# Sums of weight blocks in the second MLP product: accumulating transfers in place of GpSimd additions

## The chip, the core and the metric

The kernel runs on one core of a Trainium2 chip. Its engines work beside each other, each through its own queue in order: TensorE (PE; its weight loads are listed as PEld), VectorE (DVE), ScalarE (ACT), GpSimd (POOL), and SyncE (SP), which here only issues transfers. 16 DMA engines carry the transfers. The metric is the device time of one execution in microseconds.

## The reference

One encoder block in float32, 1024 tokens of width 1024: RMS norm, one combined projection, 2-D neighbourhood attention and a gated convolution, their gated merge, and an MLP. What the change touches is the last line, the second product:

```
h = rms_norm(x, norm2_g[l]) @ w_mlp_in[l]
x = x + jnp.square(jax.nn.relu(h)) @ w_mlp_out[l]
```

`w_mlp_out` is 4096 x 1024.

## The kernel before

Every product is made of float16 pairs: an operand is scaled, split into a high and a low half, and three passes (high x high, high x low, low x high) add up in PSUM. The big products also use a scheme of seven block products for 2 x 2 blocks in place of eight. It needs sums of blocks on both sides.

For the second MLP product the work is cut into four slices s = 0 to 3 of the inner dimension. A slice has four weight blocks w11, w12, w21, w22, each two tiles of 128 x 1024 float32 (512 KB each): w11 and w12 in four buffers `raw`, w21 and w22 in one buffer `w2x`. SP loads them from `in_weights`. The seven weight operands of a slice stand in `ORDER`: w11, then t2 = w12 + w22 + w11, then w21, then t3 = w12 + w22, then t1 = w11 + w12, then t4 = t2 + w21, then w22. t3 and t1 are made in place, in w12's and w11's buffers; t2 has a tile of its own (in slice 0 the second half of a tile `h0`, shown as h in the profile; later `t2`, shown as t). The activation sides, squared relu values and their sums, were stored to DRAM (`hs`) by the first product; they come back as `hf`, in four buffers in turn, three operands ahead (`h_load`, L1711).

`prep2(s)` makes the operands. For each one: ACT makes the high half of hf (L1765), DVE its low half (L1767); ACT makes the high half of the two weight tiles (L1770), DVE the low ones (L1776). Three operand buffers `ops` go round: `gate(i)` holds operand i back until PE is through with operand i - 3. Then follows the sum that a later operand needs: after w11, w11 += w12 (L1781, for t1); after t2, w12 += w22 (L1785, for t3); after t3, t2 += w21 (L1789, for t4). t2 is begun at the slice's start (L1739, L1740).

The consumer is the loop over 28 operands n = 7 s + o: four groups of 12 matmuls (L210), 128 x 512 each, one per 128 rows; DVE or ACT adds each result from PSUM (eight banks) to `acc` (L1866, L1864) or to the output tile `x1` (L1875). In slice 3 `combine` (L1837 to L1846) adds acc to the output on GpSimd and DVE.

The order of instructions on each engine is fixed at build time. The preparing functions are Python generators; at each matmul group the builder advances the one in front by four steps (`tick`). A `yield` is thus a place in the order and no wait. `prep2(s + 1)` stands behind `prep2(s)`. Waits come from the data alone: an instruction waits, at the head of its engine's queue, for the semaphores of what it reads or overwrites, and what stands behind it on the engine waits too.

Slice 0's preparation overlaps the end of the first product, whose sixteen quarters q leave results in tiles `as`: ACT applies relu and square (L1623, L1625), GpSimd makes four sums (L1345), SP stores them to hs (L1636).

Of the kernel before, what the change touches and what calls it, by code (L numbers as in the profile page):

```python
# [15 lines left out]
OP = mybir.AluOpType  # L16
# [36 lines left out]
def encoder_block(ctx: ExitStack, tc: tile.TileContext, x, weights, cols, gqk, rel, masks, out):  # L53
    nc = tc.nc
    V, A, G, T, SP = nc.vector, nc.scalar, nc.gpsimd, nc.tensor, nc.sync
# [27 lines left out]
    def cols_of(kind, n):  # L83
        a = area[kind]
        if a[1] + n > a[2]:
            assert kind != "keep"
            a[1] = a[0]
        a[1] += n
        return slice(a[1] - n, a[1])

    def keep(n=1):
        return cols_of("keep", n)
# [4 lines left out]
    def at(c, i, n=1):  # L97
        return slice(c.start + i, c.start + i + n)

    def mul(a, b, out=None):  # L100
        out = out or tmp(a.stop - a.start)
        V.tensor_tensor(sc[:, out], sc[:, a], sc[:, b], op=OP.mult)
        return out
# [126 lines left out]
    def load_into(t, ch, p):  # L230
        m = ch.widths[p][0] * ch.widths[p][1]
        n = m // (1 + (ch.half == 0 and p == 1))
        for o in range(0, m, n):
            SP.dma_start(t[:, o:o + n], bass.AP(tensor=weights.tensor, offset=weights.offset + ch.offs[p] + o,
                                                ap=[[m, 128], [1, n]]))

    def load_upto(n):
        while loaded[0] < min(n - held[0], limit[0], len(loads)):
            ch, p = loads[loaded[0]]
            loaded[0] += 1  # L240
            t = rawp.tile([128, 1024], F32, name="raw")
            load_into(t[:, :ch.widths[p][0] * ch.widths[p][1]], ch, p)
            ch.raw.append(t)
# [97 lines left out]
    for (kind, j), pieces in plan():  # L341
# [4 lines left out]
        for p, (k, w) in enumerate(ch.widths):  # L346
            ch.offs.append(offset)
            if kind != "X" and (kind, j) != ("1", 0) and (kind, j, p) != ("1", 1, 1):
# [3 lines left out]
    cV, cConv, cA, cB, cO, c1, c2, c2x = ([chunks[k, j] for j in range(n)] for k, n in  # L352
                                              (("V", 2), ("C", 4), ("A", 4), ("B", 4), ("O", 2),
                                               ("1", 16), ("2", 4), ("X", 4)))
# [687 lines left out]
    for k in range(N + 16):  # L1042
        p, w = k // 16, k % 16
# [71 lines left out]
    def sum_of(sm):  # L1115

        b, a = cols_of("prep", 1), ones_col()
        V.tensor_reduce(sc[:, b], sc[:, sm], axis=AX, op=OP.add)
        V.tensor_copy(a, sc[:, b])
        return a, work[0]  # L1120

    def scale_of(am, more, n=3):

        a, mark = am
        yield from apart(mark, n * 6144, work)
        b, s, inv = cols_of("prep", 1), cols_of("prep", 1), keep()
        yield from all_sum(a, b, anybank(), 1e-36)
        yield from pow2_half(b, 14, s, inv, more)
        return s, inv
# [277 lines left out]
    def gate(i):  # L1407
        while pe_done[0] < i - 2:
            yield
# [292 lines left out]
    def w2x_load(s):  # L1702
        pool = later["pool"] if s == 1 else wsp
        X2[s] = pool.tile([128, 4, 1024], F32, name="w2x", tag="w2x" if s == 1 else "ws", bufs=1 if s == 1 else 2)
        for i in range(4):
            load_into(X2[s][:, i], c2x[s], i)

    def h_load(n):
        s, f = n // 7, ORDER[n % 7][0]
        later["h", n] = later["hf"][:, n % 4]  # L1710
        SP.dma_start(later["h", n], HS[s][:, f])  # L1711
# [3 lines left out]
    def prep2(s):  # L1715
        raw, x2 = c2[s].raw, X2[s]
        w11, w12 = raw[0:2], raw[2:4]
        w21, w22 = [x2[:, i] for i in range(2)], [x2[:, i] for i in range(2, 4)]
        while not r_ready[s]:
            yield  # L1720
        Rs, iR = R[s]
        sm = cols_of("prep", 6)
        if s == 0:
            yield from gate(16)
            OPS[16] = TAGS[16 % 3][0].tile([128, 2, 2, 2048], F16, name="ops", tag=TAGS[16 % 3][1])
            j = OPS[16][:, 0, 0].bitcast(BF16)
        else:
            j = later["junk"]
        for i in range(4):
            A.activation(j[:, :1024], raw[i], AF.Square, scale=sc[:, iR], accum_out=sc[:, at(sm, i)])  # L1730
            yield
        for i in range(2):
            A.activation(j, x2[:, 2 * i:2 * i + 2].rearrange("p a c -> p (a c)"), AF.Square, scale=sc[:, iR],
                         accum_out=sc[:, at(sm, 4 + i)])
            yield
        sums = sum_of(sm)
        T2 = later["t2"]()
        for i in range(2):
            G.tensor_tensor(T2[:, i], w12[i], w22[i], op=OP.add)  # L1739
            G.tensor_tensor(T2[:, i], T2[:, i], w11[i], op=OP.add)  # L1740
        yield
        if s == 0:
            yield from gate(17)
            P = OPS[17] = TAGS[17 % 3][0].tile([128, 2, 2, 2048], F16, name="ops", tag=TAGS[17 % 3][1])
            later["h", 1] = P[:, 0].rearrange("p w m -> p (w m)").bitcast(F32).rearrange("p (k t) -> p k t", k=4)
            SP.dma_start(later["h", 1], HS[0][:, ORDER[1][0]])
        sw, inv = yield from scale_of(sums, 0)
        fw = keep()
        mul(iR, sw, fw)
        c2[s].inv = inv  # L1750
        yield
        for o, (f, name) in enumerate(ORDER):
            n = 7 * s + o
            i = 16 + n
            yield from gate(i)
            pool, tag = TAGS[i % 3]
            if n > 1:
                OPS[i] = pool.tile([128, 2, 2, 2048], F16, name="ops", tag=tag)
            P = OPS[i]
            while ("h", n) not in later:  # L1760
                yield
            if 1 < n < 25:
                h_load(n + 3)
            hf = later.pop(("h", n)).rearrange("p k t -> p (k t)")
            A.activation(P[:, 1, 0], hf, AF.Copy, scale=sc[:, Rs])  # L1765
            yield
            V.scalar_tensor_tensor(P[:, 1, 1], hf, sc[:, Rs], P[:, 1, 0], op0=OP.mult, op1=OP.subtract)  # L1767
            w = {"w11": w11, "t1": w11, "t3": w12, "w21": w21, "w22": w22}.get(name) or [T2[:, i] for i in range(2)]
            for i2 in range(2):
                A.activation(P[:, 0, 0, 1024 * i2:1024 * i2 + 1024], w[i2], AF.Copy, scale=sc[:, fw])  # L1770
            yield
            while i == 17 and pe_done[0] < 16:
                yield
            for i2 in range(2):
                sl = slice(1024 * i2, 1024 * i2 + 1024)
                V.scalar_tensor_tensor(P[:, 0, 1, sl], w[i2], sc[:, fw], P[:, 0, 0, sl], op0=OP.mult, op1=OP.subtract)  # L1776
                yield
            ready.add(i)
            if name == "w11":
                for i2 in range(2):  # L1780
                    G.tensor_tensor(w11[i2], w11[i2], w12[i2], op=OP.add)  # L1781
                yield
            elif name == "t2":
                for i2 in range(2):
                    G.tensor_tensor(w12[i2], w12[i2], w22[i2], op=OP.add)  # L1785
                yield
            elif name == "t3":
                for i2 in range(2):
                    G.tensor_tensor(T2[:, i2], T2[:, i2], w21[i2], op=OP.add)  # L1789
                yield  # L1790
            elif name == "t1":
                done[0] += 4
                load_upto(done[0] + 5)
                if s < 3:
                    w2x_load(s + 1)
                    bg.append(prep2(s + 1))
            yield
# [8 lines left out]

    bg.append(first2())
    bg.append(prep2(0))
    whole(14)
    whole(15)  # L1810
# [39 lines left out]
    for n in range(28):  # L1850
        s, o = n // 7, n % 7
# [92 lines left out]
```

## Time and profile before

| | |
|---|---|
| median of 2 runs | 1206.88 us (1206.52 to 1207.23) |
| profiled execution, span from first to last instruction | 1205.3 us |
| PE busy | 1188.0 us (99%) |
| DVE busy | 938.7 us (78%) |
| ACT busy | 759.8 us (63%) |
| POOL busy | 433.1 us (36%) |
| DMA | 173.36 MB, mean 144 GB/s |

The profiled execution's own time is the span; what lies around it isn't shown apart, and the median of the runs is 1.6 us longer. A row of a group names line, engine, operation, output and inputs, shapes and count; then busy us and the mean ns of one; then the idle time of the engine just before, and what ended it. A row of the timeline has start, duration, engine, line, operation, count, and in brackets the idle time before it with its releaser. Rows of waits and brackets put a wait for several things down to the one that came last.

### The profile page before, as it was taken

To read this page: it belongs to the slowest core of one execution; us is meant where nothing else is said; L and a number is where in the kernel's file an instruction comes from. 1 tells how busy PE (TensorE), PEld (TensorE's weight loads), DVE (VectorE), ACT (ScalarE), POOL (GpSimd) and SP (SyncE) were. 2 spreads that over 40 slices of the span, in tenths; PEclk is the share of its full clock that TensorE was granted. 3 is DMA by queue.
4 is the path that set the end of the run, shared out by engine and by line. 5 is a ranking of instruction groups with operands and counts; after the bars stand their busy time and mean duration, and the time that the engine had idled before them with its cause. 6 is when DMAs were issued, how large, how long until landed. Compare 5 with 4: busy or idle time off the path is not lost.

```text
span 1205.3 us, 17076 instructions
## 1 busy us (share of the span) xinstructions
PE 1188.0 (99%) x6294; PEld 573.8 (48%) x6294; DVE 938.7 (78%) x1759; ACT 759.8 (63%) x1183; POOL 433.1 (36%) x280
## 2 busy tenths in 40 slices
PE   6999999999999999999999999999999999999998
PEld 4444445555444444444467444444444444444444
DVE  7777988988368787877878655545548999999997
ACT  7766679867554545337779778678676744746440
POOL 1640011222311112001004465565567471553662
PEclk9999999999999999999999999999999999999999
DMA  7766657676542211224386545445465925334202
GB/s 264 151 213 141 140 119 130 133 146 123 103 123 65 67 56 53 70 93 187 57 155 183 182 159 192 149 139 193 145 247 201 352 97 217 129 138 194 105 35 105
DMA packets 171012, 173.36 MB, mean 144 GB/s; under 512 B 131504, under 2 KB 132016, under 8 KB 166832
## 3 DMA queue, kind: packets, MB, share of 16 engines
q1 hardware_dynamic: 170352, 168.07, 47.9%
q10 hardware_dynamic: 576, 4.19, 0.8%
q8 instruction: 49, 0.80, 0.3%
q14 instruction: 35, 0.29, 0.1%
HBM read 102.51 MB, written 37.75 MB: 116 GB/s over the span
## 4 chain that ended last, share of the span: by engine, by line
PE 73%; DVE 9%; ACT 1%; issue 1%; DMA 1%; DVEq 0%; ACTq 0%
PE ps_d L210 26%; PE ps_s L210 23%; PE ps_o L210 16%; PE ps_d L1039 6%; DVE w_s L1163 2%; PE ps_o L1016 1%; PE ps_s L959 1%; DVE sg L1279 1%; DVE P L999 1%; DMA u2T<-v 1%; DVE sz L973 1%; ACT w_s L1167 0%; DVE sc L317 0%; DVE m L1281 0%; ACT sg L1245 0%
## 5 line engine op out<-in xcount | busy, mean ns | idle before, releaser
L210 PEld LDWEIGHTS <-ops 128*128 128x128 f16 x1356 | 132.4, 98 | 157.3
L210 PEld LDWEIGHTS <-w 128*128 128x128 f16 x1368 | 132.8, 98 | 140.0 <-DMA u2T<-v 0.6
L1039 PE MATMUL ps_d<-uT,w_ws 128*128 128x512 f16 x528 | 123.7, 379 | 0.1
L210 PE MATMUL ps_d<-ops 128*128 128x512 f16 (+1 forms) x528 | 118.3, 374 | 0.0
L1765 ACT ACTIVATE ops<-hf,sc 128x2048 f16<-128x2048 f32 x26 | 52.0, 2000 | 97.9 <-PE ps_o L210 35.2
L210 PE MATMUL ps_s<-ops 128*128 128x512 f16 x492 | 112.9, 379 | 0.0
L1152 POOL TENSOR_TENSOR tsum<-raw 128x512 f32<-128x512 f32 x28 | 46.0, 1658 | 149.6 <-ACT raw L1138 141.6
L1345 POOL TENSOR_TENSOR as<-as 128x512 f32<-128x512 f32 x56 | 77.5, 1384 | 39.3 <-ACT as L1625 36.0
L210 PEld LDWEIGHTS <-w_s 128*128 128x128 f16 x588 | 56.8, 98 | 69.4 <-DVE w_s L1163 1.9
L210 PE MATMUL ps_d<-u2x,w 128*128 128x512 f16 (+1 forms) x360 | 80.0, 372 | 0.0
L210 PEld LDWEIGHTS <-uT 128*128 128x128 f16 x504 | 49.0, 98 | 59.6 <-DMA uT<-u 0.8
L1039 PEld LDWEIGHTS <-w_ws 128*128 128x128 f16 x528 | 51.2, 98 | 54.5 <-DVE cv L861 0.4
L210 PE MATMUL ps_o<-ops 128*128 128x512 f16 x336 | 77.1, 379 | 0.0
L1767 DVE SCALAR_TENSOR_TENSOR ops<-hf,sc,ops 128x2048 f16<-128x2048 f32 x26 | 74.0, 2846 | 3.7 <-ACT ops L1765 3.7
L210 PE MATMUL ps_o<-u2T,w 128*128 128x512 f16 (+1 forms) x324 | 71.7, 371 | 0.0
L1138 ACT ACTIVATE raw<-raw,sc 128x256 f32<-128x256 f32 x172 | 71.0, 493 | 0.8 <-DMA raw<-in_weights 0.7
L1152 POOL TENSOR_TENSOR gsum<-raw 128x512 f32<-128x512 f32 x14 | 19.0, 1376 | 133.0 <-issue 72.8
L1167 ACT ACTIVATE w<-raw,sc 128x512 f16<-128x512 f32 (+1 forms) x28 | 24.6, 927 | 54.1 <-DVE sc L426 54.1
L297 DVE SCALAR_TENSOR_TENSOR w_ws<-raw,sc,w_ws 128x512 f16<-128x512 f32 (+2 forms) x72 | 51.2, 763 | 4.7 <-ACT w_ws L306 4.7
L1658 DVE TENSOR_TENSOR as<-ps_d,as 128x512 f32<-128x512 f32 (+1 forms) x14 | 9.4, 672 | 55.8 <-ACT as L1677 53.4
L210 PE MATMUL ps_s<-u2T,w 128*128 128x512 f16 (+1 forms) x252 | 52.7, 359 | 0.0
L982 ACT ACTIVATE sz<-sz,sc 128x384 f32<-128x384 f32 (+1 forms) x64 | 37.2, 582 | 22.5 <-DVE sc L973 15.0
(357 smaller groups left out, 2629.5 us busy)
## 6 DMA issues: line engine op xcount, KB each, us to landing
raw<-in_weights SPq DMA_DIRECT2D x88, 512.0 KB, 5.4
hs<-as SPq DMA_DIRECT2D x16, 1792.0 KB, 8.7
hf<-hs SPq DMA_DIRECT2D x26, 1024.0 KB, 6.3
w2x<-in_weights SPq DMA_DIRECT2D x16, 512.0 KB, 8.1
raw<-in_weights SPq DMA_DIRECT2D x16, 384.0 KB, 3.5
xt<-in_x SPq DMA_DIRECT2D x8, 512.0 KB, 10.0
gs<-s ACTq DMA_DIRECT2D x4, 1024.0 KB, 4.0
x<-in_x SPq DMA_DIRECT2D x8, 512.0 KB, 9.8
```

Of the source, the lines that this page charges most:

```text
L210: T.matmul(ps, l, r, start=a, stop=b)
L297: V.scalar_tensor_tensor(lo, self.raw[p][:, o:o + m], sc[:, c:c + 1], hi, op0=OP.mult, op1=OP.subtract)
L959: T.matmul(ps[:, :nb * 128], QD[:, p, e, w, i * 128:(i + 1) * 128], KD[:, 2 * p + e, lo * 128:(lo + nb) * 128], start=w == 0, stop=w == 1)
L982: A.activation(z, z, AF.Exp, scale=-1.0, bias=sc[:, d["mx"]], accum_out=sc[:, d["sm"]])
L1039: T.matmul(ps, l, r, start=a, stop=b)
L1138: A.activation(v, v, AF.Copy, scale=sc[:, at(g, 4 * i + k)])
L1152: G.tensor_tensor(t[:, o], a, b, op=OP.add)
L1163: V.scalar_tensor_tensor(o(1), w, sc[:, s], o(0), op0=OP.mult, op1=OP.subtract)
L1167: A.activation(o(0), w, AF.Copy, scale=sc[:, s])
L1345: sub.tensor_tensor(z[o], z[a], z[b], op=op)
L1765: A.activation(P[:, 1, 0], hf, AF.Copy, scale=sc[:, Rs])
L1767: V.scalar_tensor_tensor(P[:, 1, 1], hf, sc[:, Rs], P[:, 1, 0], op0=OP.mult, op1=OP.subtract)
```

## The change

The additions that make t2, t1, t3 and t4 in `prep2` become transfers from SBUF to SBUF that add to their destination (`accum_op`), issued from GpSimd's queue. t2's start value is no longer made by an addition: w12 is loaded from `in_weights` a second time, straight into t2's tile, by SP (`load_into`). Then w22 and w11 are added to it, one pair of transfers each, with a step of the order between.

```diff
         sums = sum_of(sm)
         T2 = later["t2"]()
         for i in range(2):
-            G.tensor_tensor(T2[:, i], w12[i], w22[i], op=OP.add)
-            G.tensor_tensor(T2[:, i], T2[:, i], w11[i], op=OP.add)
-        yield
+            load_into(T2[:, i], c2[s], 2 + i)
+        yield
+        for w in w22, w11:
+            for i in range(2):
+                G.dma_start(T2[:, i], w[i], accum_op=OP.add)
+            yield
...
             if name == "w11":
                 for i2 in range(2):
-                    G.tensor_tensor(w11[i2], w11[i2], w12[i2], op=OP.add)
+                    G.dma_start(w11[i2], w12[i2], accum_op=OP.add)
                 yield
             elif name == "t2":
                 for i2 in range(2):
-                    G.tensor_tensor(w12[i2], w12[i2], w22[i2], op=OP.add)
+                    G.dma_start(w12[i2], w22[i2], accum_op=OP.add)
                 yield
             elif name == "t3":
                 for i2 in range(2):
-                    G.tensor_tensor(T2[:, i2], T2[:, i2], w21[i2], op=OP.add)
+                    G.dma_start(T2[:, i2], w21[i2], accum_op=OP.add)
                 yield
```

The order on PE, ACT and DVE stays as it was. On GpSimd the transfers take the places of the additions. On SP each slice has two loads more: in slice 0 between the store of quarter 13's sums and the load of hf for operand 1, in the later slices behind the loads of hf for operands 7 s + 1 and 7 s + 2.

## The prediction

> **What bounds the kernel now.** First the page's busy shares: who is full?
>
> ```profile
> span 1205.3 us, 17076 instructions
> ...
> PE 1188.0 (99%) x6294; PEld 573.8 (48%) x6294; DVE 938.7 (78%) x1759; ACT 759.8 (63%) x1183; POOL 433.1 (36%) x280
> ```
>
> TensorE is. Then the windows of the two last stages, 640 to 904 (first MLP product) and 904 to 1198 (second one, where the changed sums are used). Columns: busy us of PE, PEld, DVE, ACT, POOL, granted clock, DMA share, GB/s.
>
> ```profile
> 640.00:904.00 264.00, 264.00 (x1314) 127.34 (x1313) 152.06 (x308) 201.70 (x291) 150.81 (x107) 1.00 0.52 176
> 904.00:1198.00 294.00, 294.00 (x1366) 133.32 (x1365) 278.61 (x247) 146.93 (x132) 153.83 (x54) 1.00 0.43 159
> ```
>
> In the second stage PE is busy 294.00 of 294 us at clock 1.00: it waits for nothing. DVE is close behind (278.61). Last the chain that ended last, at its end:
>
> ```profile
> 1196.26 2.59 PE ps_o L210 x12
> 1198.85 2.63 PE ps_d L210 x24
> 1201.48 0.03 issue
> 1201.51 0.48 DVE x L1875
> ```
>
> It is PE to 1201.48, then one eviction and a store. So a faster GpSimd or DVE shortens nothing here; the change can only keep PE at work or make it wait. When must an operand be ready? PE's first group of operand 0, and of operand 10:
>
> ```profile
> 911.12 2.75 PE L210 MATMUL ps_s<-ops 128*128 128x512 f16 x12
> 1014.75 2.75 PE L210 MATMUL ps_o<-ops 128*128 128x512 f16 x12
> ```
>
> (1014.75 - 911.12)/10 = 10.36 us an operand: operand n starts at 911.1 + 10.36 n. A slice s has seven of them (72.5 us): w11, t2, w21, t3, t1, t4, w22.
>
> **What goes.** GpSimd's sums, by line:
>
> ```profile
> L1781 POOL TENSOR_TENSOR raw<-raw 128x1024 f32<-128x1024 f32 x8 | 30.8, 3869 | 35.7 <-DVE ops L1776 35.7
> L1785 POOL TENSOR_TENSOR raw<-raw,w2x 128x1024 f32<-128x1024 f32 x8 | 25.6, 3217 | 0.0
> L1789 POOL TENSOR_TENSOR t<-t,w2x 128x1024 f32<-128x1024 f32 x6 | 21.5, 3605 | 0.0
> L1739 POOL TENSOR_TENSOR t<-raw,w2x 128x1024 f32<-128x1024 f32 x6 | 18.0, 2992 | 63.9 <-DMA w2x<-in_weights 63.9
> L1740 POOL TENSOR_TENSOR t<-t,raw 128x1024 f32<-128x1024 f32 x6 | 16.9, 2825 | 0.5
> ...
> L1789 POOL TENSOR_TENSOR h<-h,w2x 128x1024 f32<-128x1024 f32 x2 | 6.6, 3342 | 0.0
> L1740 POOL TENSOR_TENSOR h<-h,raw 128x1024 f32<-128x1024 f32 x2 | 4.7, 2359 | 0.2
> L1739 POOL TENSOR_TENSOR h<-raw,w2x 128x1024 f32<-128x1024 f32 x2 | 4.7, 2358 | 0.0
> ```
>
> (The last three are slice 0's, where t2 lies in tile h.) Together some 129 us of GpSimd work leave. DVE gains too. Its weight splits (min/median/max ns):
>
> ```profile
> L1776 DVE SCALAR_TENSOR_TENSOR ops<-w2x,sc,ops x16: 1271/2179/3384, 927.1 to 1186.5; 128x1024 f16<-128x1024 f32 x16
> ```
>
> 1271 ns alone, up to 3384 beside GpSimd. [...] But PE hides DVE's time already (294.00 of 294), so I price this gain at 0; it shows only as later slack.
>
> **What comes: the price of a transfer.** Each pair of additions becomes a pair of accumulating transfers of 512 KB, 40 in all; and SP loads t2's start value (w12) again, 2 x 512 KB a slice. Call D the time from a pair's first issue to the landing of its second. No accumulating transfer is in this trace. The nearest rows are copies of 1 MB, which is what a pair writes (KB, median us to landing; then min/median/max of the hf loads):
>
> ```profile
> ops<-hs SPq DMA_DIRECT2D x1, 1024.0 KB, 4.7
> hs<-as SPq DMA_DIRECT2D x16, 1792.0 KB, 8.7
> ...
> DMA to landing us min/median/max: 4.6/6.3/15.6
> ```
>
> And DMA when it is full (columns as above):
>
> ```profile
> 953.00:966.00 13.00, 13.00 (x62) 5.93 (x61) 8.64 (x9) 12.84 (x15) 7.00 (x3) 1.00 1.01 412
> ```
>
> A plain copy of 1 MB takes 4.7 in quiet; an accumulation also reads the destination, another 1.05 MB, at the 412 GB/s of saturated DMA 2.5 us; two issues of some 0.4 make 0.8 (SP's issues below take 0.53 for a store, 4.30/4 for loads in a row; on GpSimd none is shown, so from 0 to the 2.36 of the addition that it replaces). Together **D = 8 us**, an estimate. From below it is 4.7 (the second read free), from above 15.6 (as slow as the worst queued load of 1 MB). I take 8 as nearest to the quiet row, since the critical ones fall into quiet stretches.
>
> [...]
>
> **Where it lands: slice 0.** GpSimd's queue and SP's issues around it:
>
> ```profile
> 886.75 2.36 POOL L1739 TENSOR_TENSOR h<-raw,w2x 128x1024 f32<-128x1024 f32 x1
> ...
> 898.73 8.11 POOL L1345 TENSOR_TENSOR as<-as 128x512 f32<-128x512 f32 x4 [2.42 <-ACT as L1625]
> 906.80 7.71 POOL L1781 TENSOR_TENSOR raw<-raw 128x1024 f32<-128x1024 f32 x2
> ...
> 886.82 0.53 SPq L1636 DMA_DIRECT2D hs<-as  x1
> ...
> 906.86 0.53 SPq L1636 DMA_DIRECT2D hs<-as  x1
> 907.48 4.30 SPq L1711 DMA_DIRECT2D hf<-hs  x4
> ```
>
> In the changed program SP issues the load of t2 right behind the hs store of 886.82; GpSimd's w22 pair waits for it, the w11 pair for the w22 pair, and behind the w11 pair stands the as sums of 898.73 (quarter 14 of the first product), then its store, then the hf loads. So:
> - The load is queued behind the 1.8 MB store (8.7 us): 886.8 + 8.7 = 895.5. Alone it would be 888 + 4.7 = 892.7.
> - w22 pair landed at 895.5 + 8 = 903.5; issuing the w11 pair 1 us: GpSimd is free at 904.5, not 898.7. **+5.8 us** for the as sums, the store and the hf loads.
> - Then w11 += w12 (the 906.80 row) is in flight beside these loads: 1.05 MB more at the 309 GB/s below is **+3.4 us** (from 0 to twice that).
>
> ```profile
> 907.00:919.00 12.00, 12.00 (x57) 5.46 (x56) 11.97 (x10) 2.41 (x3) 12.00 (x4) 1.00 0.93 309
> ```
>
> Does operand 2 bear that? Its chain:
>
> ```profile
> 912.38 2.19 ACT L1770 ACTIVATE ops<-h,sc 128x1024 f16<-128x1024 f32 x2 [7.38 <-DVE ops L1767]
> 918.78 2.00 ACT L1765 ACTIVATE ops<-hf,sc 128x2048 f16<-128x2048 f32 x1 [4.21 <-DMA hf<-hs]
> ...
> 924.69 2.00 ACT L1625 ACTIVATE as<-as,sc 128x2048 f32<-128x2048 f32 x1
> ...
> 926.82 0.16 DVE L1640 TENSOR_REDUCE sc<-sc 128x1 f32<-128x4 f32 x1 [3.35 <-ACT as L1625]
> ...
> 929.20 2.23 DVE L1776 SCALAR_TENSOR_TENSOR ops<-w2x,sc,ops 128x1024 f16<-128x1024 f32 x1
> ```
>
> ACT waits for the hf load until 918.78, does hf, the weights, then relu and square of quarter 15; DVE's reduce waits for that, and its last split of operand 2 ends at 929.20 + 2.23 = 931.43. PE wants operand 2 at 911.1 + 20.7 = 931.8: slack 0.4. Everything in this chain is in order on ACT and DVE, so 5.8 + 3.4 - 0.4 = **8.8 us of PE idle** at operand 2. Later operands shift with it. t2 itself (w11 pair landed near 911.5) is in time for ACT, which reads it at 912.4.
>
> **Slices 1 to 3.** Here a chain replaces the adds: load of t2, w22 pair, w11 pair, then w11 += w12, then w12 += w22 (t3), four D. t3 must be whole some 4 us before its PE start (ACT 2.2 for both halves, DVE 1.3 for the last).
>
> ```profile
> 958.92 3.42 POOL L1739 TENSOR_TENSOR t<-raw,w2x 128x1024 f32<-128x1024 f32 x1 [16.48 <-DMA w2x<-in_weights]
> ...
> 966.00:976.00 10.00, 10.00 (x49) 4.55 (x48) 9.20 (x19) 5.99 (x6) 3.46 (x2) 1.00 0.07 16
> ```
>
> Slice 1: DMA is full to 966 (1.01 above), then idle (0.07). Another 1 MB for t2, behind two hf loads on SP, and slice 0's t4 sum make it some 970. t2 is whole at 970 + 16 = 986, wanted by 994 - 4 = 990; t3 at 970 + 32 = 1002, wanted by 1014.7 - 4 = 1010.7. Hidden, to D = 10.2. Slices 2 and 3: the t2 load waits until DVE has read the old t2 (1019.25 + 2.47 = 1021.7 in slice 2), lands near 1029; t3 at 1061, wanted by 1087.3 - 4 = 1083. Hidden, to D = 13.6.
>
> ```profile
> 1019.25 2.47 DVE L1776 SCALAR_TENSOR_TENSOR ops<-t,sc,ops 128x1024 f16<-128x1024 f32 x2
> ```
>
> DMA capacity: a slice moves about 159 GB/s x 72.5 us = 11.5 MB; 10 transfers that count twice add 10.5 and the t2 load 1.05: 23 MB, 318 GB/s against 412. It fits, with less room.
>
> **Sum.** 1205.3 + 8.8 = 1214.1 for the profiled execution, which stands 1.6 under the median of 1206.9; so **1216 us**.
>
> **Rivals.**
> 1. All hidden: D near 4.7, the load at 892.7, no contention. GpSimd is free at 898 and PE never waits: 1207. For it: the quiet copy of 4.7. Against: the store ahead in SP's queue.
> 2. Slower than before by more than 2%: the transfers are slow, and t3's four-link chain binds in every slice. From D = 12.5 on: 10.3 + 4 - 0.4 = 14 us in slice 0 and 4 x (12.5 - 10.2) = 9 in slice 1, 23 us. At D = 15.6: 13.4 + 6.8 - 0.4 = 20 in slice 0, 22 in slice 1, 8 in each of slices 2 and 3: 58 us, 1265. For it: no row shows an addition inside a transfer. Against: that it needs the rate of a queued load in a quiet stretch.
> 3. GpSimd can't issue while DVE runs, so that the work doesn't leave it: each pair waits for one or two DVE instructions of 1.3 to 3.4 us. At 5 us more, D = 13, the time is 1233. DVE's 278.6 of 294 speak for it; that GpSimd's 2.36 us additions ran beside DVE in this trace speaks against. [...]
> 4. Faster by over 2%: PE would have to do without work that it has; only the 3.8 us behind 1201.5 aren't PE's. No mechanism that I see.
>
> **Chances.** Forecast (PE waits 1.5 to 23 us, mostly once) 0.52; rival 1 0.18; rival 2 0.25; rival 3 0.03; rival 4 0.02. A measurement of this kernel tells about 2% from no change: above 1231 is slower. So faster 0.02, same 0.70, slower 0.28. Range: from 1206.5 (half of rival 1 below) to 1250, which is D = 14.5; beyond it about 0.10.
>
> **What the changed profile would show.** Right: PE's only new idle time in 904 to 1198 is near operand 2 (about 932 to 941), released by DVE's split behind the hf load; the as sums start near 904; DVE's splits of 1.3 us where they were 2.3; GpSimd's busy time 130 us less; t2, t3 in time from slice 1 on. Wrong: ACT or DVE waiting on GpSimd's queue for t or raw in each slice (rival 2), or issues on GpSimd of several us (rival 3). The forecast falls if an accumulation's price lies outside 4.7 to 12, or if the load of t2 overtakes the store.

## The result, and the profile after

The changed kernel takes 1217.28 us (median of 2 runs, 1217.18 to 1217.37) against 1206.88: a ratio of 1.0086, 95% interval 1.0056 to 1.0115, 10.4 us slower. The forecast was 1216 us. Below the mechanism is taken apart, since errors in the forecast's sum cancel in part.

Behind line 1744 the lines of the changed program stand three higher: ACT's high halves of hf and of the weights, L1765 and L1770 before, are L1768 and L1773, and DVE's, L1767 and L1776, are L1770 and L1779. The additions that begin t2 (L1739, L1740) are now transfers issued by L1743.

The page's head, the changed kernel:

```profile
span 1215.6 us, 17136 instructions
...
PE 1191.2 (98%) x6294; PEld 574.7 (47%) x6294; DVE 889.2 (73%) x1759; ACT 759.9 (63%) x1183; POOL 335.9 (28%) x280
```

DVE lost 49.5 us of work and GpSimd 97.2, and the span grew by 10.3. The window of the second product's stage, 904 to 1208, with the columns of the prediction (PE, PEld, DVE, ACT, POOL busy, granted clock, DMA share, GB/s):

```profile
904.00:1208.00 304.00, 296.61 (x1363) 133.71 (x1362) 229.96 (x247) 146.56 (x132) 67.03 (x57) 0.98 0.78 229
```

PE had no gap here; now it has 304 - 296.61 = 7.4 us. The DMA share went from 0.43 to 0.78. What PE waited for on L210 from 850 us on (columns: total, times, longest):

```profile
PE ps_s L210 <- ACT acc L1867: 6.1, 1, 6.1
PE ps_s L210 <- DVE ops L1779: 1.3, 1, 1.3
```

Two waits, once each. PE's timeline, from operand 0 and then at operand 2:

```profile
910.68 2.75 PE L210 MATMUL ps_s<-ops 128*128 128x512 f16 x12
...
928.81 2.75 PE L210 MATMUL ps_d<-ops 128*128 128x512 f16 x12
937.69 0.59 PE L210 MATMUL ps_s<-ops 128*128 128x512 f16 x1 [6.12 <-ACT acc L1867]
939.54 4.85 PE L210 MATMUL ps_s<-ops 128*128 128x512 f16 x11 [1.27 <-DVE ops L1779]
944.19 3.21 PE L210 MATMUL ps_o<-ops 128*128 128x512 f16 x12
947.24 2.75 PE L210 MATMUL ps_d<-ops 128*128 128x512 f16 x12
```

Operand 0 starts at 910.68. Operand 2 should start 20.72 later, at 931.40, and its third group at 936.58; that group starts at 947.24. So 10.7 us are lost at one place: 7.4 in the two waits, and 3.3 outside them, nearly all in matmuls that are slow, as the granted clock shows (windows, same columns):

```profile
929.00:935.00 6.00, 2.56 (x12) 1.07 (x11) 2.35 (x1) 5.91 (x5) 0.00 (x0) 0.99 1.04 309
935.00:945.00 10.00, 6.04 (x14) 2.02 (x14) 7.84 (x9) 10.00 (x13) 7.62 (x4) 0.50 0.58 205
946.00:950.00 4.00, 4.00 (x20) 1.81 (x19) 4.00 (x3) 3.61 (x3) 1.81 (x3) 1.00 0.70 221
```

From 935 to 945 the clock is 0.50: PE's pause is followed by a stretch at half speed, which no gap in PE's busy time shows. From 939.54 to about 945.1, 5.6 us, PE works at that clock before it is 1.00 again. The last section compares the runs on this.

Why operand 2 is late, from the chain that ended last:

```profile
913.67 15.30 DMA hf<-hs
...
929.06 2.00 ACT ops L1768
931.06 2.08 ACT ops L1773 x2
933.14 1.81 ACT as L1623
...
934.97 2.10 ACT as L1625 x2
...
937.44 2.06 DVE ops L1779
...
939.54 4.85 PE ps_s L210 x11
```

It is the predicted chain: hf load, hf's high half, the weights, relu and square, DVE's split, PE. The load is issued at 913.67 and ACT starts on it at 929.06. Before the change these were 907.48 and 918.78. Counted from operand 0's start (910.68 and 911.12), the issue is 6.6 us later and the load 15.4 us long where it was 11.3: hf is 10.7 us late. And why the issue is late, from GpSimd's timeline:

```profile
896.48 1.93 POOL L1743 DMA_DIRECT2D h<-w2x  x2 [10.13 <-DMA h<-in_weights]
902.26 0.86 POOL L1743 DMA_DIRECT2D h<-raw  x1 [3.85 <-DMA h<-w2x]
904.85 0.88 POOL L1743 DMA_DIRECT2D h<-raw  x1 [1.73 <-DMA h<-w2x]
905.41 7.62 POOL L1345 TENSOR_TENSOR as<-as 128x512 f32<-128x512 f32 x4
912.97 1.75 POOL L1784 DMA_DIRECT2D raw<-raw  x2
```

GpSimd stands still for 10.13 us until t2's load has landed, then 3.85 and 1.73 more for the w22 transfers, with the as sums behind: they start at 905.41, not 898.73 (7.1 us later, counted from operand 0). The row 912.97 is the pair w11 += w12, in flight beside the hf load.

### The profile page after: what moved, and what is told of

Same layout as the page of the kernel before. It is cut to its first block, busy times and chain, and to the rows that moved or that the text cites. A ratio compares the mean times of both kernels' runs of the same rounds, so it can differ in the third digit from the quotient of the medians.

```text
span 1215.6 us, 17136 instructions
## 1 busy us (share of the span) xinstructions
PE 1191.2 (98%) x6294; PEld 574.7 (47%) x6294; DVE 889.2 (73%) x1759; ACT 759.9 (63%) x1183; POOL 335.9 (28%) x280
## 4 chain that ended last, share of the span: by engine, by line
PE 60%; DVE 9%; ACT 3%; DMA 2%; issue 2%; POOL 0%; SPq 0%; DVEq 0%; ACTq 0%; POOLq 0%
PE ps_d L210 24%; PE ps_s L210 21%; PE ps_o L210 15%; DVE w_s L1163 2%; DMA hf<-hs 1%; DVE sg L1279 1%; DMA u2T<-v 1%; ACT w_s L1167 0%; ACT as L1623 0%; DMA PT<-P 0%; DVE sc L317 0%; DVE ops L1779 0%; DVE m L1281 0%; DVE w L1163 0%; ACT sg L1245 0%
## 5 line engine op out<-in xcount | busy, mean ns | idle before, releaser
L210 PEld LDWEIGHTS <-ops 128*128 128x128 f16 x1356 | 133.1, 98 | 167.3 <-issue 11.7
L210 PEld LDWEIGHTS <-w 128*128 128x128 f16 x1368 | 132.8, 98 | 140.0 <-DMA u2T<-v 0.6
L210 PE MATMUL ps_s<-ops 128*128 128x512 f16 x492 | 115.6, 385 | 7.4 <-ACT acc L1867 6.1
L210 PE MATMUL ps_d<-ops 128*128 128x512 f16 (+1 forms) x528 | 118.3, 374 | 0.0
L1768 ACT ACTIVATE ops<-hf,sc 128x2048 f16<-128x2048 f32 x26 | 52.0, 1998 | 91.7 <-PE ps_o L210 54.3
L210 PEld LDWEIGHTS <-w_s 128*128 128x128 f16 x588 | 56.7, 98 | 69.4 <-DVE w_s L1163 1.9
L1770 DVE SCALAR_TENSOR_TENSOR ops<-hf,sc,ops 128x2048 f16<-128x2048 f32 x26 | 62.8, 2414 | 30.2 <-ACT ops L1768 30.2
L210 PE MATMUL ps_d<-u2x,w 128*128 128x512 f16 (+1 forms) x360 | 80.0, 372 | 0.0
L210 PE MATMUL ps_o<-ops 128*128 128x512 f16 x336 | 77.5, 381 | 0.0
L210 PEld LDWEIGHTS <-uT 128*128 128x128 f16 x504 | 49.0, 98 | 59.4 <-DMA uT<-u 0.7
L210 PE MATMUL ps_o<-u2T,w 128*128 128x512 f16 (+1 forms) x324 | 71.7, 371 | 0.0
L210 PE MATMUL ps_s<-u2T,w 128*128 128x512 f16 (+1 forms) x252 | 52.7, 359 | 0.0
```

The lines of the kernel that those rows point to most:

```text
L210: T.matmul(ps, l, r, start=a, stop=b)
```

## Experiments

Theory 1 is the prediction's: all of the loss arises in slice 0, out of a hold of GpSimd's queue and a load in company. Against it stand: the long chain of t3 in slices 1 to 3; the traffic of the transfers as such; a rule by which the order on GpSimd doesn't matter. Differences are against the kernel before on the same chip (1206.90 for the first four, 1207.27 for the next four, 1207.04 for the last).

**Which slice: transfers in slices 1 to 3 alone.**

```diff
+        if s > 0:
...
+                load_into(T2[:, i], c2[s], 2 + i)
...
+        else:
+            for i in range(2):
+                G.tensor_tensor(T2[:, i], w12[i], w22[i], op=OP.add)
+                G.tensor_tensor(T2[:, i], T2[:, i], w11[i], op=OP.add)
             yield
...
             if name == "w11":
                 for i2 in range(2):
-                    G.dma_start(w11[i2], w12[i2], accum_op=OP.add)
+                    if s > 0:
+                        G.dma_start(w11[i2], w12[i2], accum_op=OP.add)
+                    else:
+                        G.tensor_tensor(w11[i2], w11[i2], w12[i2], op=OP.add)
...
```

(The lines left out at `...` are the two pairs for s > 0, and the same choice for the other two later sums.)

> Slice 0 is made with GpSimd's additions as before, slices 1 to 3 with transfers. Theory 1 (the loss is made in slice 0 alone: GpSimd's queue held ahead of quarter 14's sums, and a crowded hf load for operand 2): 1206 to 1208 us, PE without a pause near operand 2, DVE's weight splits of slices 1 to 3 at 1.3 us and still no gain. Theory 2 (the transfers cost in every slice, by DMA load or GpSimd's issues; three of four slices keep them): some 1214 us.

1207.27 us, ratio 1.0002 (0.9993 to 1.0011). The stage's window:

```profile
904.00:1198.00 294.00, 294.00 (x1367) 133.35 (x1365) 239.70 (x247) 146.75 (x132) 76.35 (x54) 1.00 0.74 223
```

Three quarters of the change are in, DVE is down from 278.61 to 239.70 us, GpSimd from 153.83 to 76.35, the DMA share is 0.74, and PE is as full as before: no loss, and no gain either. The rival of the long chain falls.

**Transfers in slice 0 alone** (the same edit with `s == 0`).

> Only slice 0 is made with transfers, slices 1 to 3 with additions. Theory 1: the whole loss stays, 1216 to 1218 us. Theory 2: a quarter of it, some 1209 us.

1217.81 us, 1.0089 (1.0075 to 1.0103): the whole loss.

**The two halves of slice 0.** First: t2 begun by additions, the later sums by transfers. Then the other way round.

```diff
+        if s > 0:
...
+        else:
+            for i in range(2):
+                G.tensor_tensor(T2[:, i], w12[i], w22[i], op=OP.add)
+                G.tensor_tensor(T2[:, i], T2[:, i], w11[i], op=OP.add)
```

> In slice 0 only t2's start (the load and two pairs) goes back to additions; w11 += w12, w12 += w22 and t2 += w21 stay transfers, slices 1 to 3 too. Theory 1: GpSimd reaches quarter 14's sums at 898 as before, and what is left is the transfer beside the hf load (hf landing about 4 us later, less 0.4 of slack): PE waits 3 to 4 us, 1210 to 1212 us with what the clock adds after a pause. If the held queue were all of it: 1207. If the crowded load were all of it: 1217.

1211.69 us, 1.0040 (1.0028 to 1.0053), as expected. The as sums start at 899.17, on time (operand 0 at 911.58). What is left is the hf load beside w11 += w12, issued at 907.93:

```profile
924.93 2.00 ACT L1774 ACTIVATE ops<-hf,sc 128x2048 f16<-128x2048 f32 x1 [11.42 <-DMA hf<-hs]
```

924.93 - 907.93 = 17.0 us for a load that took 11.3. That part alone makes hf 5.7 us late and costs 4.8 us.

> In slice 0 t2's start stays with transfers (load and two pairs); the three later sums go back to additions. Theory 1: GpSimd reaches quarter 14's sums some 7 us late, the hf load then takes its 11 us: PE waits 6 to 7 us, 1213 to 1216 us. If the held queue were all of it: 1217. If the crowded load were all of it: 1207.

1211.86 us, 1.0043 (1.0030 to 1.0055), a little under the expected 1213 to 1216. Here the as sums are held to 905.46, the load is issued at 913.71, and it is not crowded:

```profile
924.07 2.00 ACT L1768 ACTIVATE ops<-hf,sc 128x2048 f16<-128x2048 f32 x1 [12.61 <-DMA hf<-hs]
```

10.4 us, less than before the change; so the hold of 7.1 us reaches ACT as 5.6, and costs 5.0. PE waits 2.5 us, where 6 to 7 were expected: the expectation still took the slack as 0.4 us. The two halves cost 4.8 + 5.0 = 9.8 of 10.4 (of 10.9 with slice 0 alone, on the same chip). That they nearly add up is in part chance, since each has the whole slack for itself and a stretch at half speed of its own.

**The hold without any transfer.** The kernel before, with the first addition of slice 0's t2 done four times more on GpSimd.

```diff
+        for _ in range(4 if s == 0 else 0):
+            G.tensor_tensor(T2[:, 0], w12[0], w22[0], op=OP.add)
```

> The kernel before, with no transfer, and four more additions (each a repeat of the first of t2, 2.36 us) in slice 0 on GpSimd ahead of t2's own: 9.4 us less the 2.4 us that GpSimd idles there holds quarter 14's sums back by 7.0 us, as the changed kernel does (7.1). Theory 1 (it is the held queue, not that a transfer holds it): as e4, PE stops for 2 to 3 us at operand 2, then runs at half clock for some 3 us, 1211 to 1213 us. Rival (the loss is in the transfers themselves, their issues or their traffic): 1207.

1215.89 us, 1.0069 (1.0056 to 1.0083): the direction as expected, the size a miss, because the last addition took 4.28 us where the three before it took 2.36 to 2.37, and the as sums 9.10 where they took 8.11 before the change (GpSimd's timeline; what stretched them was not shown):

```profile
886.75 9.67 POOL L1739 TENSOR_TENSOR h<-raw,w2x 128x1024 f32<-128x1024 f32 x4
...
903.69 4.28 POOL L1742 TENSOR_TENSOR h<-h,raw 128x1024 f32<-128x1024 f32 x1
907.93 9.10 POOL L1345 TENSOR_TENSOR as<-as 128x512 f32<-128x512 f32 x4
```

Counted from operand 0 (911.13), the as sums are 9.2 us late and hf 9.3. PE waits 5.4 us at operand 2, and 0.6 at operand 1, since t2 is late here too. The loss is 8.6 us (9.4 in the profiled execution), with no transfer added anywhere. To hold what stands behind on GpSimd's queue is enough; that the hold is a wait for a DMA isn't needed for the loss.

**Shortening the hold: t2's load ahead of the store.** In the changed kernel, SP issues slice 0's t2 load before the store of 887.

```diff
-        for i in range(2):
+        for i in range(2 if s else 0):
             load_into(T2[:, i], c2[s], 2 + i)
...
+        T2 = later["t2"]()
+        for i in range(2):
+            load_into(T2[:, i], c2[0], 2 + i)
```

> The changed kernel, with slice 0's load of t2 issued some 11 us earlier, ahead of quarter 13's store. Theory 1: the w22 pair starts when GpSimd is through with quarter 13's sums (886), the w11 pair near 895, quarter 14's sums start at 898 as before; what is left is the w11 += w12 transfer beside the hf load, as in e3: 1211 to 1212 us. If the place of the load did not matter: 1217.

1217.48 us, 1.0084 (1.0070 to 1.0097): a miss. The load landed 6.7 us earlier (counted from operand 0, at 911.91 here), but so the w22 pair flew beside the store of 1.8 MB:

```profile
890.97 1.02 POOL L1743 DMA_DIRECT2D h<-w2x  x1 [3.38 <-DMA h<-in_weights]
892.14 0.87 POOL L1743 DMA_DIRECT2D h<-w2x  x1 [0.15 <-issue]
899.38 0.86 POOL L1743 DMA_DIRECT2D h<-raw  x1 [6.37 <-DMA h<-w2x]
903.83 0.88 POOL L1743 DMA_DIRECT2D h<-raw  x1 [3.59 <-DMA h<-w2x]
904.39 9.31 POOL L1345 TENSOR_TENSOR as<-as 128x512 f32<-128x512 f32 x4
```

890.97 to 903.83: the pair takes 12.9 us, against 8.4 (896.48 to 904.85) in the changed kernel. The hold shrinks by 2.2 us only, and slower sums (9.31 for 7.62) take most of that back. The expectation moved a transfer and kept its price, and the time came out as if the place of the load did not matter; the hold of 4.9 us for 7.1 shows that it does, a little.

**The same with slice 0's later sums as additions**, which was to remove both parts.

> e6 (t2's load early, its start by transfers) with the three later sums of slice 0 by additions; slices 1 to 3 by transfers. Theory 1: neither the held queue nor the crowded load is left, 1206 to 1209 us. If transfers in slice 0 cost by themselves: 1211 or more.

1211.47 us, 1.0034 (1.0021 to 1.0046): a miss for the same reason, and equal to the second half alone (1211.86). Nothing crowds the hf load (10.3 us); the hold remains, 4.9 us. The time is also the one that the rival had named (transfers in slice 0 cost by themselves, 1211 or more), so this run alone doesn't tell the two apart; the run with GpSimd held, which loses as much and more without a transfer, does.

**How long may the chain be in slice 1?** Slices 1 to 3 by transfers, as in the first run, and in slice 1 a third pair into t2 (t2 then has w11 twice, and the output differs). The edit, against the first run:

```diff
-            for w in w22, w11:
+            for w in (w22, w11, w11) if s == 1 else (w22, w11):
```

> e1 (slice 0 with additions, slices 1 to 3 with transfers), and in slice 1 a third pair of transfers into t2 (w11 once more, so that t2 and the output differ from the reference's). In e1 the second half of t2's weights is split at 987.2 and PE starts operand 8 at 993.7: 6.4 us to spare. A pair takes 8 to 10 us there. Theory 1 (a transfer costs only what exceeds the time to spare): PE waits 2 to 4 us at operand 8, with half clock behind it 1209 to 1213 us. If the chain were hidden anyway: 1207. If every pair cost its length: 1216.

1207.55 us, 1.0002 (0.9994 to 1.0011): a miss. t2's last split ended at 987.25 in the first run and ends here at 992.77 + 1.28 = 994.05. A link costs 6.8 us, not 8 to 10: the two tiles of a pair are two chains, and a tile's next link starts when that tile has landed (the third pair's issues, at 977.82 and 984.37, had each waited for t<-raw, 1.76 and 5.69 us). PE starts the operand at 993.7 and needs its second tile only some 1.5 us later (seven of the first twelve matmuls come before, see below), so nothing waits.

**Taking the hold away with all transfers kept.** In slice 0 the pair t2 += w11 is issued behind the as sums.

```diff
-        for w in w22, w11:
+        for w in (w22, w11) if s else (w22,):
...
             if name == "w11":
+                for i2 in range(0 if s else 2):
+                    G.dma_start(T2[:, i2], w11[i2], accum_op=OP.add)
```

> The changed kernel, but in slice 0 the pair t2 += w11 is issued behind the sums of the first product's quarter 14 (as sums) and ahead of w11 += w12; all sums are still made by transfers, the output is the same. Theory 1 (loss = held sums + crowded hf load): the w22 pair is issued when t2's load lands (near 896.5), so GpSimd is free by 898 and the as sums start at 898 to 899 as before the change: the held part, 7.1 us, goes. Two pairs now fly beside the hf load instead of one, so the load takes 17 us or more (17.0 in the run that had the second half alone), at most some 22: hf of operand 2 is split 5.5 to 10 us late, 1212 to 1217 us. Rival (the place of the pair in GpSimd's queue doesn't matter, the loss is the total traffic of slice 0's transfers): the time stays at 1217 with the as sums anywhere.

1213.60 us, 1.0053 (1.0036 to 1.0070). The as sums start at 899.26, on time, so the place in the queue decides about the hold. The hf load, now beside two pairs, takes 17.2 us and is 5.9 late. But PE loses only 3.4 us at operand 2, and 2.6 elsewhere; 0.5 more lies ahead of operand 0. PE's timeline:

```profile
929.79 2.75 PE L210 MATMUL ps_d<-ops 128*128 128x512 f16 x12
933.89 0.38 PE L210 MATMUL ps_s<-ops 128*128 128x512 f16 x1 [1.34 <-ACT acc L1869]
934.88 1.46 PE L210 MATMUL ps_s<-ops 128*128 128x512 f16 x6 [0.62 <-DVE ops L1779]
937.30 1.24 PE L210 MATMUL ps_s<-ops 128*128 128x512 f16 x5 [0.96 <-DVE ops L1779]
...
969.45 2.75 PE L210 MATMUL ps_s<-ops 128*128 128x512 f16 x12
974.60 0.18 PE L201 MATMUL ps_o<-ones 128*128 128x1 bf16 x1 [2.39 <-DVE ones L1119]
```

The wait of 2.39 us at 974.60 is a new one. This small matmul spreads the scale of slice 1's weights; DVE's row L1119 before it comes from ACT's pass over those weights. ACT waits for their load, and before that, at 956.20, it had waited 3.03 us for t4's transfer:

```profile
969.51 2.00 ACT L1733 ACTIVATE junk<-w2x,sc 128x2048 bf16<-128x2048 f32 x1 [0.94 <-DMA w2x<-in_weights]
...
972.06 2.00 ACT L1733 ACTIVATE junk<-w2x,sc 128x2048 bf16<-128x2048 f32 x1 [0.46 <-DMA w2x<-in_weights]
```

So the number fell in the expected range while half of its mechanism was another: with the first stall made shorter, the crowded DMA (share 1.03 from 945 to 980) shows at the next consumer.

All runs in one table. "Late" is against the kernel before, counted from operand 0's start; "load" is from the issue of the hf load to ACT's start on it.

| run | as sums late | load | hf late | PE waits | loss |
|---|---|---|---|---|---|
| before | 0 | 11.3 | 0 | 0 | 0 |
| t2 begun by additions | 0.0 | 17.0 | 5.7 | 3.1 | 4.8 |
| later sums by additions | 7.1 | 10.4 | 5.6 | 2.5 | 5.0 |
| load early, later sums by additions | 4.9 | 10.3 | 5.1 | 2.8 | 4.2 |
| GpSimd held, no transfer | 9.2 | 10.4 | 9.3 | 6.0 (0.6 of it at operand 1) | 8.6 |
| load early | 4.9 | 15.2 | 10.0 | 6.7 | 10.2 |
| changed kernel | 7.1 | 15.4 | 10.7 | 7.4 | 10.4 |
| w11 pair behind the sums | 0.0 | 17.2 | 5.9 | 2.9 | 6.6 |

The loss is that of the medians; the other columns are from the profiled execution, at operand 2 where nothing else is said. In every row PE waits 2.3 to 3.3 us less than hf is late, so there is more slack than 0.4 us. Most of what the loss has above the waits is the clock at 0.50 behind them; in the last row it is slice 1's scale. In the row "load early, later sums by additions" the clock stayed at 1.00; its profiled execution has a span of 1209.1, 3.8 longer than before: 3.3 at operand 2, and 0.5 ahead of operand 0, which starts at 911.62. No version beats the kernel before, as none can while PE has no gap to fill; the best of them, with slice 0 left alone, equals it.

## Why the prediction was right, and where it wasn't

- **What bounds the kernel: right.** With the stage's DVE and GpSimd work cut by 39 and 77 us in the first run, the time stays. The gain on DVE, priced at 0, is there and is worth 0:

```profile
L1779 DVE SCALAR_TENSOR_TENSOR ops<-w2x,sc,ops 128x1024 f16<-128x1024 f32 x16 | 21.7, 1390 | 0.0
```

  1390 ns where these splits took 2307 (36.4 us for the same 16).
- **D = 8: right in the quiet stretch** (8.4), but not one number: 12.9 beside the store. The bounds of 4.7 to 15.6 held. That an accumulation reads its destination too (the sum's 2.5 us, and the transfers that count twice in the DMA capacity) no run shows by itself; the runs show the two pairs' times, and 202 GB/s at a full share of DMA where plain copies reached 412 (below). "Four D" for t3 is an upper bound, since tiles go on singly.
- **The load of t2 behind the store, landed 895.5: right** (896.48).
- **The hold, +5.8: 7.1.** Counted from operand 0, the load was 1.4 later than worked out and D 0.4 longer; the issue took less.
- **The crowded load, +3.4: too small.** The load is 4.1 longer than before, and 5.7 in the run that has the pair alone. At its new place it takes 10.4 when nothing crowds it (later sums by additions), so the pair costs 15.4 - 10.4 = 5.0. The sum divided its 1.05 MB by the 309 GB/s of plain traffic; at the 202 GB/s of accumulating transfers shown below it is 5.2.
- **The slack, 0.4: the step that failed.** It was read at the end of DVE's last split of operand 2 (931.43, for a start at 931.84). But PE doesn't need that split at the start. The split of the operand's first half, in the kernel before:

```profile
927.08 2.13 DVE L1776 SCALAR_TENSOR_TENSOR ops<-w2x,sc,ops 128x1024 f16<-128x1024 f32 x1
```

  It ends at 929.21. PE's rows in the last run show one matmul, then six, and then the wait for the second half: seven of twelve matmuls, 1.5 us, come before it. So the second half may end 931.84 + 1.5 - 931.43 = 1.9 us later, and the first, wanted by the second matmul at 932.06, 2.8 us later. At full clock the second is the tighter: with the load early and the later sums by additions, hf was 5.1 us late and PE lost 3.3 at operand 2. With a slack of 1.9 the sum's own 9.2 us of lateness would have given 7.3 instead of 8.8, and the measured 10.7 gives 8.8.
- **The clock: not in the sum.** PE lost 10.7 us at operand 2, so half speed behind the pause makes it 10.7 - 8.8 = 1.9 us more than the lateness alone would. (At half speed PE comes to the second half only when it is there, so the trace shows the late first half, 10.7 - 2.8 = 7.9, and 2.8 of slow matmuls.)
- **Luck in the sum.** The 1.5 us of lateness that the two parts lacked and the 1.5 us of slack overlooked cancel; the clock's 1.9 remain. The span of 1215.6 stands only 1.5 above the sum of 1214.1 because operand 0 starts 0.4 earlier in that execution. The mechanism was right; that the number came so close is in part luck.
- **Slices 1 to 3 hidden: right, with less margin than worked out.** The first run shows it free. In the changed kernel the 4 us that the prediction had left for slice 1's t2 are gone (timeline, with ACT, DVE and PE):

```profile
1001.73 1.15 ACT L1773 ACTIVATE ops<-t,sc 128x1024 f16<-128x1024 f32 x1 [4.19 <-DMA t<-raw]
...
1002.91 1.28 DVE L1779 SCALAR_TENSOR_TENSOR ops<-t,sc,ops 128x1024 f16<-128x1024 f32 x1 [4.06 <-ACT ops L1773]
...
1004.24 0.59 PE L210 MATMUL ps_o<-ops 128*128 128x512 f16 x2
```

  The last split ends at 1004.19 and PE starts the operand at 1004.24; since it needs this half only 1.5 us later, some 1.6 us are left. The two pairs took from 981.8 to 1001.7, 19.9 us in full DMA (share 1.03), where 16 were assumed. And the load of slice 1's weights, which no step named, is the next to bind, together with t4's transfer ahead of it, as the last run shows.
- **Rivals.** All hidden: refuted by the two halves of slice 0, each of which costs. The slow chain: refuted by the first run. GpSimd unable to issue beside a busy DVE: refuted, no issue takes more than 1.2 us (most 0.86 to 0.9), with DVE busy 230 of 304 us.
- **The signs.** PE's only gap near operand 2: right (931.56 to 939.54); released by DVE's split, with ACT's eviction (L1867), which stands behind relu and square, ending the longer part. The as sums near 904: 905.4. GpSimd 130 us less: 97.2, since 40 issues of 0.87 us, 35 in all, count as busy.

## What to carry to other kernels

Moving work from an engine to a transfer frees the engine's time (here 97.2 us of GpSimd), but can put a wait for an earlier transfer at the head of the queue that issues it (here 10.13, 3.85 and 1.73 us); look at what is queued behind the issue and how much slack that has, not at the engine's busy time. A transfer has no fixed price (a pair took 8.4 us in a quiet stretch and 12.9 beside a store): work out what flies beside it at its new place, and look for the next consumer of the same DMA time. When a full TensorE gets a pause, look at the granted clock behind it (here it was 0.50 for 3.4 to 10.2 us after stops of 2.9 us and more), and count the slack for each part of an operand from the matmul that reads it first.

## What the runs showed of the hardware

Accumulating transfers filled the DMA engines with half the bytes of plain copies. From 900 to 904 of the changed kernel, with the pairs into t2 in flight (windows; before the change nothing is moved in this stretch):

```profile
900.00:904.00 4.00, 4.00 (x21) 1.77 (x19) 3.39 (x2) 4.00 (x4) 0.86 (x1) 1.00 1.03 202
```

202 GB/s at a share of 1.03, where plain copies, from 953 to 966 of the kernel before, reached 412 at 1.01.

The clock also fell where a matmul stood within PE's stop. With later sums by additions PE stood from 931.66 to 934.55 with a single matmul of 0.38 us between, and the clock fell:

```profile
935.00:938.00 3.00, 3.00 (x8) 1.02 (x7) 2.97 (x4) 3.00 (x3) 2.84 (x3) 0.50 0.00 0
```

With the load early as well it stood 2.4 us in the same manner (932.5 to 934.9), and the clock stayed:

```profile
935.00:938.00 3.00, 2.24 (x11) 0.89 (x10) 2.97 (x4) 3.00 (x3) 2.92 (x2) 1.00 0.00 0
```

Both runs wait 2.5 to 2.8 us in all, so it is not the sum of the waits that decides. With t2 begun by additions it was 2.9 us and the clock fell; with the w11 pair behind the sums 2.3, and it stayed. So in these few runs the clock fell behind stops of 2.9 us and more, and stayed at 1.00 behind 2.3 and 2.4; what it is at lengths between, and whether it also matters when the pause begins, stays open.

The stretches at half speed had three lengths in these traces. The mean clock of a window gives the part of it at 0.50. Window by window, from where the clock falls to where it is 1.00 again:

| run | windows, us | mean clock of each | at 0.50, us |
|---|---|---|---|
| t2 begun by additions | 936 to 940, by 1 | 0.75, 0.50, 0.50, 0.55 | 3.4 |
| later sums by additions | 934 to 939, by 1 | 0.95, 0.50, 0.50, 0.50, 0.84 | 3.4 |
| slice 0 alone | 937 to 945, by 2 | 0.56, 0.50, 0.50, 0.74 | 6.8 |
| load early | 936 to 944, by 4 | 0.51, 0.64 | 6.8 |
| changed kernel | 933 to 947, by 2 | 0.97, 0.50 five times, 0.97 | 10.2 |

With GpSimd held it is 0.80 from 937 to 938 and 0.50 from 938 to 943; PE's twelve matmuls from 943.23 then take 3.35 us where such a group takes 2.75 at full clock, which puts the end near 944.4, again 6.8 us. The clock fell 3.2 to 4.9 us after PE's pause began; with t2 begun by additions that is at 936.5, when PE has been at work again for 1.1 us. The length of the stop doesn't settle it: the changed kernel and the run of slice 0 alone stop PE for 8.0 and 7.8 us and run 10.2 and 6.8 at half speed. Each is read from one trace, and what picks the length wasn't tested.
